# A decoder block's gate and up products: one pair of k-tiles by seven block products instead of eight

## The chip, the core and the metric

The kernel runs on one core of a Trainium2 chip. The metric is the device time of one execution in microseconds (us); less is better. The engines are PE (TensorE: matmuls, and PEld for its weight loads), DVE (VectorE), ACT (ScalarE), POOL (GpSimd) and SP (SyncE, which here issues the loads of weights).

## What is computed

A decoder block on 256 tokens of width 2048 in float32: attention and an mLSTM side by side, a SwiGLU feed-forward stage, and a gated per-layer embedding. What the change touches is the first half of the feed-forward stage, with weights of 2048 x 5632:

```python
h2 = rms_norm(x, w_norm_ffn[i])
x = x + (jax.nn.silu(h2 @ w_ffn_gate[i]) * (h2 @ w_ffn_up[i])) @ w_ffn_down[i]
gate = jax.nn.sigmoid(rms_norm(x, w_norm_ple[i]) @ w_ple_gate[i])
```

## The kernel before

**Split operands.** The matmuls take operands of type fp32r. Each operand is a sum of two parts: a cast by ACT (wh, act_h) and the rest by a DVE subtraction (wl, act_l). A product takes three matmuls, high x high, high x low and low x high (lines 255 to 257), each with a 128x128 block of activations as weights of PE and 512 columns of the weight matrix streaming through it. The activations lie transposed, contraction on the partitions: a "k-tile" is 128 of the 2048 contraction rows, a "block" b is 128 of the 256 tokens.

**One linear (lines 210 to 258).** It walks over pieces of two k-tiles. SP loads a piece of 128x1024 floats (wr), ACT casts it (L230), DVE subtracts (L231), and PE multiplies each of its k-tiles with both blocks into two PSUM banks (acc0, acc1): 12 matmuls for each piece. wr, wh and wl have four buffers each. PSUM has four names (acc0, acc1, tr, sc) with two banks each, eight in all.

**Feed-forward (lines 644 to 659).** The 5632 columns are 11 chunks of 512. A chunk is a linear for gate, per block a sigmoid by ACT (L650) and a DVE product (L651), a linear for up, and per block one more DVE product (L654): 2 x 16 x 2 x 3 = 192 matmuls. Then a task turns the chunk's result into activations for the down product: DVE transposes of 32x32 into "tq" (L187), four POOL DMAs to DRAM ("swap", L191), one back into "quad" (L196), then cast and subtraction (L129, L130). "tq" and "quad" have one buffer each, and a list `held` lets one task at a time use them. The activations of the chunk before the first (acts_h, four quarters of four k-tiles) are made in the same way after each quarter of the attention output product; PE needs the last quarter for k-tiles 12 to 15.

**What sets the order.** Python writes the instructions in order; the background tasks write a step whenever `advance` is called, once for each piece here. A planner then puts each engine's instructions in an order of its own: on each engine it takes the earliest written one that is ready by its estimate of the times. On the chip that order is fixed: a DVE or ACT instruction that waits holds everything queued behind it.

**Before down.** Lines 660 to 664 load p, transpose it on PE and split it, between the last chunk and the first down piece. `e_norm` loads w_ple_post into one buffer (wpost, L679).

Of the kernel before, what the change touches and what calls it, by code (L numbers as in the profile page):

```python
# [19 lines left out]
def block_kernel(ctx, tc, x, p, w_norm_mix, w_in, fox_f_bias, q_norm_w, k_norm_w, conv_w, conv_b,  # L20
# [180 lines left out]
    def split_by_blocks(dst, srcs, scales=None, gap=2):  # L201
# [5 lines left out]
                yield  # L207
        held.pop()

    def linear(w, acts, c0, n, pieces=None, before=None, load=None, width=2):  # L210

        po = [ps.tile([P, 512], F32, name=f"acc{b}") for b in range(2)]
        total = w.shape[0] // P
        if pieces is None:
            step = 1024 // n if n < 512 else 2
            pieces = [(k, min(step, total - k)) for k in range(0, total, step)]
        count = 0
        ready = []

        def fetch(i):  # L220
            kt, nk = pieces[i]
            if load is not None:
                load(kt)

            def piece(name, dt):
                return wpool.tile([P, 1024], dt, name=name)[:, 0:nk * n].rearrange("p (k n) -> p k n", k=nk)

            wr, wh, wl = piece("wr", F32), piece("wh", F32R), piece("wl", F32R)
            nc.sync.dma_start(out=wr, in_=w[kt * P:(kt + nk) * P, c0:c0 + n].rearrange("(k p) n -> p k n", p=P))
            nc.scalar.copy(wh, wr)  # L230
            nc.vector.tensor_tensor(wl, wr, wh.bitcast(F32), op=ALU.subtract)  # L231
            ready.append((wh, wl))

        for i, (kt, nk) in enumerate(pieces):
            if before is None:
                advance(width)
                fetch(i)
            else:
                if i == 0:
                    fetch(0)  # L240
                    before(kt)
                if i + 1 < len(pieces):
                    fetch(i + 1)
                if i:
                    before(kt)
            wh, wl = ready[i]
            for j in range(nk):
                ah, al = acts[(kt + j) // 4]
                while id(ah) in made_by and not made_by[id(ah)].done:
                    advance(2)  # L250
                kk = (kt + j) % 4
                count += 1
                for b in range(2):
                    s = slice(b * P, (b + 1) * P)
                    nc.tensor.matmul(po[b][:, 0:n], ah[:, kk, s], wh[:, j, :], start=count == 1, stop=False)  # L255
                    nc.tensor.matmul(po[b][:, 0:n], ah[:, kk, s], wl[:, j, :], start=False, stop=False)  # L256
                    nc.tensor.matmul(po[b][:, 0:n], al[:, kk, s], wh[:, j, :], start=False, stop=count == total)  # L257
        return [t[:, 0:n] for t in po]


    with tc.tile_pool(name="mixp", bufs=1) as mp:
# [52 lines left out]
        def qk_norm(s, dT, vec):  # L314
            ss = small.tile([P, 2, 4], F32, name="ss_qk")
            rr = small.tile([P, 2, 4], F32, name="r_qk")
            for b in range(2):
                sq = small.tile([P, 512], F32, name="sqf", bufs=1)
# [319 lines left out]
    with tc.tile_pool(name="ffnp", bufs=1) as fp:  # L638
        acts_g = []

        def after_up(dst, gg):
            yield from split_by_blocks(dst, lambda b: gg[b])

        for c in range(NG):
            pg = linear(w_gate, acts_h, c * 512, 512, width=1)
            gg = [None, None]
            for b in range(2):
                gg[b] = fp.tile([P, 512], F32, name=f"gg{b}", bufs=2)
                r = rstd2[:, b:b + 1]
                nc.scalar.activation(gg[b], pg[b], AF.Sigmoid, scale=r)  # L650
                nc.vector.scalar_tensor_tensor(gg[b], pg[b], r, gg[b], op0=ALU.mult, op1=ALU.mult)  # L651
            pu = linear(w_up, acts_h, c * 512, 512, width=1)
            for b in range(2):
                nc.vector.scalar_tensor_tensor(gg[b], pu[b], rstd2[:, b:b + 1], gg[b], op0=ALU.mult, op1=ALU.mult)  # L654
# [5 lines left out]
        p_sb = fp.tile([P, 512], F32, name="gg0", bufs=2).rearrange("p (b k) -> p b k", b=2)  # L660
        nc.sync.dma_start(out=p_sb, in_=p.rearrange("(b p) k -> p b k", p=P))
        acts_p = (fp.tile([P, 2, 256], F32R, name="ph"), fp.tile([P, 2, 256], F32R, name="pl"))
        for _ in transpose_in(acts_p, lambda b, j: p_sb[:, b, j * P:(j + 1) * P], 0, 2):
            pass
        e = []

        def e_norm():
            ss_e = const.tile([P, 2, 4], F32, name="ss_e")
            rstd_e = const.tile([P, 2], F32, name="rstd_e")
            for c in range(4):  # L670
                for b in range(2):
                    sumsq(ss_e[:, b, c:c + 1], e[c][:, b, :])
                yield
            ssr = small.tile([P, 2], F32, name="ssr")
            nc.vector.tensor_reduce(ssr, ss_e, axis=AX.X, op=ALU.add)
            rsqrt(rstd_e, ssr, 1.0 / D, [P, 2])
            for c in range(4):
                cs = slice(c * 512, (c + 1) * 512)
                wpost = fp.tile([P, 512], F32, name="wpost")  # L679
                nc.sync.dma_start(out=wpost, in_=w_ple_post[0, cs].partition_broadcast(P))  # L680
                for b in range(2):
                    yield
                    nc.vector.scalar_tensor_tensor(e[c][:, b, :], e[c][:, b, :], rstd_e[:, b:b + 1], wpost,
                                                   op0=ALU.mult, op1=ALU.mult)

        def e_chunks():
            for c in range(4):
                po = linear(w_ple_proj, [acts_p], c * 512, 512)
                e.append(act.tile([P, 2, 512], F32, name="act_h"))
                for b in range(2):  # L690
                    nc.scalar.copy(e[c][:, b, :], po[b])
            Task(e_norm())

        order = [(k, 2) for k in list(range(16, 4 * NG, 2)) + list(range(0, 16, 2))]
        acts_h3, rstd3 = residual(w_down, acts_g, v_ple, "ple", pieces=order)


        e_chunks()
        out_v = out.rearrange("(b p) n -> p b n", p=P)
        for c0, n in ((0, 512), (512, 512), (1024, 512), (1536, 256), (1792, 256)):  # L700
            cs = slice(c0, c0 + n)
            po = linear(w_ple_gate, acts_h3, c0, n)
            for b in range(2):
                g = fp.tile([P, 512], F32, name=f"gg{b}", bufs=2)[:, 0:n]
# [32 lines left out]
```

## Time and profile before

| | us |
|---|---|
| median of 3 runs (1227.53 to 1228.53) | 1228.31 |
| the profiled execution | 1228.32 |
| its span, first to last instruction | 1226.6 |
| PE / DVE / ACT busy | 1215.5 / 713.4 / 585.9 |

Times are counted from the start of the span. PE's busy time counts pipelined matmuls that overlap, so it says when PE has something to do, not that it is at its peak; the distance between the starts of neighbouring matmuls says that. In the waits, "A <- B" is an engine's line that stood still until B's was done, and the idle time of an engine that is not the bottleneck costs nothing. In a timeline, a bracket tells how long the engine stood before the instruction, and what released it; "x2" is two of them merged. Gate and up run from 400 to 880 us.

### The profile page before, as it was taken

To read this page: it belongs to the slowest core of one execution; us is meant where nothing else is said; L and a number is where in the kernel's file an instruction comes from. 1 tells how busy PE (TensorE), PEld (TensorE's weight loads), DVE (VectorE), ACT (ScalarE), POOL (GpSimd) and SP (SyncE) were. 2 spreads that over 40 slices of the span, in tenths; PEclk is the share of its full clock that TensorE was granted. 3 is DMA by queue.
4 is the path that set the end of the run, shared out by engine and by line. 5 is a ranking of instruction groups with operands and counts; after the bars stand their busy time and mean duration, and the time that the engine had idled before them with its cause. 6 is when DMAs were issued, how large, how long until landed. Compare 5 with 4: busy or idle time off the path is not lost.

```text
span 1226.6 us, 15283 instructions
## 1 busy us (share of the span) xinstructions
PE 1215.5 (99%) x5675; PEld 1018.3 (83%) x5675; DVE 713.4 (58%) x956; ACT 585.9 (48%) x766; POOL 79.5 (6%) x149
## 2 busy tenths in 40 slices
PE   8999999999999999999999999999999999999998
PEld 6899978878888788888888888888888888888888
DVE  5766755665656655555565565555545554545754
ACT  6655556545545444444444444444444444446542
POOL 1111000000010000000000000000000000000000
PEclk9999999999999999999999999999999999999999
DMA  7677744675677776776776677677666666665672
GB/s 260 205 237 230 231 139 130 177 236 170 207 247 243 222 223 197 233 223 195 230 228 209 209 231 226 191 230 229 210 212 208 213 208 212 205 212 168 220 248 90
DMA packets 136383, 257.32 MB, mean 210 GB/s; under 512 B 10002, under 2 KB 29300, under 8 KB 136308
## 3 DMA queue, kind: packets, MB, share of 16 engines
q1 hardware_dynamic: 127156, 229.06, 59.6%
q0 software_dynamic: 8400, 26.22, 6.8%
q8 instruction: 44, 0.72, 0.2%
q10 hardware_dynamic: 752, 1.06, 0.2%
q14 instruction: 31, 0.25, 0.1%
HBM read 241.10 MB, written 15.20 MB: 209 GB/s over the span
## 4 chain that ended last, share of the span: by engine, by line
PE 91%; DMA 4%; DVE 2%; ACT 1%; issue 1%; POOL 0%; SPq 0%; DVEq 0%; ACTq 0%; POOLq 0%
PE acc L256 30%; PE acc L255 30%; PE acc L257 30%; DMA quad<-swap 2%; DMA wr<-in_w_in_dram 1%; DVE wl L231 1%; DMA swap<-tq 1%; ACT wh L230 0%; PE tr L165 0%; POOL swap L191 0%; PE sc L552 0%; PE tr L569 0%; DVE tq L187 0%; PE sc L505 0%; PE tr L489 0%
## 5 line engine op out<-in xcount | busy, mean ns | idle before, releaser
L231 DVE TENSOR_TENSOR wl<-wr,wh 128x1024 fp32r<-128x1024 f32 (+2 forms) x445 | 525.0, 1182 | 435.9 <-ACT wh L230 434.8
L230 ACT CAST wh<-wr 128x1024 fp32r<-128x1024 f32 (+2 forms) x445 | 452.2, 1019 | 558.1 <-PE acc L257 522.8
L255 PE MATMUL acc<-wh,act_h 128*128 128x512 f32 (+2 forms) x1568 | 594.0, 379 | 2.3 <-ACT act_h L133 2.3
L256 PE MATMUL acc<-wl,act_h 128*128 128x512 f32 (+2 forms) x1568 | 591.1, 377 | 1.2 <-DVE wl L231 1.2
L257 PE MATMUL acc<-wh,act_l 128*128 128x512 f32 (+2 forms) x1568 | 591.3, 377 | 0.0
L255 PEld LDWEIGHTS acc<-wh,act_h 128*128 128x128 f32 x1568 | 294.8, 188 | 54.5 <-ACT act_h L133 3.5
L256 PEld LDWEIGHTS acc<-wl,act_h 128*128 128x128 f32 x1568 | 294.8, 188 | 52.1 <-DVE wl L231 1.9
L257 PEld LDWEIGHTS acc<-wh,act_l 128*128 128x128 f32 x1568 | 294.7, 188 | 52.0 <-DVE act_l L135 0.8
L191 POOL DMA_DIRECT2D swap<-tq x100 | 61.0, 616 | 877.0 <-DVE tq L187 877.0
L255 PE MATMUL acc<-wh,gh 128*128 128x512 f32 x224 | 88.0, 393 | 0.0
L256 PE MATMUL acc<-wl,gh 128*128 128x512 f32 x224 | 87.9, 393 | 0.0
L257 PE MATMUL acc<-wh,gl 128*128 128x512 f32 x224 | 87.1, 389 | 0.0
L257 PEld LDWEIGHTS acc<-wh,gl 128*128 128x128 f32 x224 | 42.0, 188 | 9.5
L255 PEld LDWEIGHTS acc<-wh,gh 128*128 128x128 f32 x224 | 42.1, 188 | 9.4
L256 PEld LDWEIGHTS acc<-wl,gh 128*128 128x128 f32 x224 | 42.1, 188 | 8.6
L196 POOL DMA_DIRECT2D quad<-swap x25 | 14.0, 559 | 114.0 <-DMA swap<-tq 69.1
L650 ACT ACTIVATE gg<-acc,rstd_ffn 128x512 f32<-128x512 f32 x22 | 15.1, 689 | 10.8 <-PE acc L257 10.8
L651 DVE SCALAR_TENSOR_TENSOR gg<-acc,rstd_ffn,gg 128x512 f32<-128x512 f32 x22 | 15.8, 751 | 5.0 <-ACT gg L650 5.0
L133 ACT ACTIVATE act_h<-quad,vec_b 128x256 fp32r<-128x256 f32 x32 | 13.7, 498 | 4.5 <-DMA quad<-swap 4.3
L654 DVE SCALAR_TENSOR_TENSOR gg<-acc,rstd_ffn,gg 128x512 f32<-128x512 f32 x22 | 15.4, 744 | 0.0
L135 DVE SCALAR_TENSOR_TENSOR act_l<-quad,vec_b,act_h 128x256 fp32r<-128x256 f32 x32 | 13.4, 480 | 2.9 <-ACT act_h L133 2.9
L116 ACT ACTIVATE sq<-xres 128x512 bf16<-128x512 f32 x24 | 14.9, 623 | 0.0
(194 smaller groups left out, 405.1 us busy)
## 6 DMA issues: line engine op xcount, KB each, us to landing
wr<-in_w_ffn_gate_dram SPq DMA_DIRECT2D x88, 512.0 KB, 3.8
wr<-in_w_ffn_up_dram SPq DMA_DIRECT2D x88, 512.0 KB, 4.5
wr<-in_w_ffn_down_dram SPq DMA_DIRECT2D x88, 512.0 KB, 4.0
wr<-in_w_in_dram SPq DMA_DIRECT2D x63, 512.0 KB, 4.7
wr<-in_w_in_dram SPq DMA_DIRECT2D x48, 344.0 KB, 3.7
wr<-in_w_out_dram SPq DMA_DIRECT2D x32, 512.0 KB, 4.5
wr<-in_w_ple_gate_dram SPq DMA_DIRECT2D x32, 512.0 KB, 4.7
swap<-tq POOLq DMA_DIRECT2D x100, 128.0 KB, 4.4
```

The lines of the kernel that those rows point to most:

```text
L116: nc.scalar.activation(sq[:, 0:n], src, AF.Square, accum_out=dst)
L133: nc.scalar.activation(part(dst[0], k + j, 1), src[:, j:j + 1], AF.Copy, scale=scales[j])
L191: nc.gpsimd.dma_start(out=d[:, :, :, i, :].rearrange("j c b e -> c b j e"), in_=t[32 * i:32 * i + 32].rearrange("c b j k r -> c b j (k r)"))
L196: nc.gpsimd.dma_start(out=q.rearrange("p t k r -> p (t k r)"), in_=d.rearrange("j c b i e -> (j c) (b i e)"))
L230: nc.scalar.copy(wh, wr)
L231: nc.vector.tensor_tensor(wl, wr, wh.bitcast(F32), op=ALU.subtract)
L255: nc.tensor.matmul(po[b][:, 0:n], ah[:, kk, s], wh[:, j, :], start=count == 1, stop=False)
L256: nc.tensor.matmul(po[b][:, 0:n], ah[:, kk, s], wl[:, j, :], start=False, stop=False)
L257: nc.tensor.matmul(po[b][:, 0:n], al[:, kk, s], wh[:, j, :], start=False, stop=count == total)
L650: nc.scalar.activation(gg[b], pg[b], AF.Sigmoid, scale=r)
L651: nc.vector.scalar_tensor_tensor(gg[b], pg[b], r, gg[b], op0=ALU.mult, op1=ALU.mult)
L654: nc.vector.scalar_tensor_tensor(gg[b], pu[b], rstd2[:, b:b + 1], gg[b], op0=ALU.mult, op1=ALU.mult)
```

## The change

Gate and up of a chunk are now done together (`gate_up`). A pair of k-tiles is a unit: its gate and up pieces side by side are a 2x2 block matrix (rows: the two k-tiles, columns: gate and up), and the activations of the pair another (rows: the two token blocks, columns: the k-tiles). Seven of the eight pairs are multiplied plainly, in eight block products. One pair, k-tiles 2 and 3 (`seven = (1,)`), which comes fifth in the first chunk and fourth in the others, is multiplied by Strassen's scheme (in Winograd's form): seven products P1 to P7 of sums of blocks. The sums of the activations are made once by a task (`make_forms`, into fh and fl), those of the weights in every chunk by DVE (`seven_unit`: t12, t34, in a two-buffer tile "wt"), and each is cast and split like a piece (`halves`), in 3.5 pieces instead of 2. The plain products go straight into the banks of P2, P3, P4 and P8; P1, P5, P6 and P7 have four banks of their own, are read in mid chunk (`t1`, `qr`, `su`) and added to the others at the chunk's end. The four shared banks and the four own ones change names from chunk to chunk. `qr` lies in "quad" and `su` in "tq". gg0 and gg1 have one buffer instead of two, p is loaded and transposed by a task during the down product, sqf moves to another pool, and wpost gets two buffers.

```diff
+    def halves(wr):
+        k, n = wr.shape[1:]
+        wh, wl = (wpool.tile([P, 1024], F32R, name=name)[:, 0:k * n].rearrange("p (k n) -> p k n", k=k)
+                  for name in ("wh", "wl"))
+        nc.scalar.copy(wh, wr)
+        nc.vector.tensor_tensor(wl, wr, wh.bitcast(F32), op=ALU.subtract)
+        return wh, wl
...
-            wr, wh, wl = piece("wr", F32), piece("wh", F32R), piece("wl", F32R)
-            nc.sync.dma_start(out=wr, in_=w[kt * P:(kt + nk) * P, c0:c0 + n].rearrange("(k p) n -> p k n", p=P))
-            nc.scalar.copy(wh, wr)
-            nc.vector.tensor_tensor(wl, wr, wh.bitcast(F32), op=ALU.subtract)
-            ready.append((wh, wl))
+            ready.append(halves(load_piece(w, kt, nk, c0, n)))
...
+        seven = (1,)
+        first_order, later_order = (0, 2, 3, 4, 1, 5, 6, 7), (0, 2, 3, 1, 4, 5, 6, 7)
+        def make_forms(p):
+            while held:
+                yield held
+            held.append(p)
...
+            fa = quads.tile([P, 2, 2, P], F32, name="tq")
...
+            nc.vector.tensor_tensor(fa.rearrange("p k b t -> p k (b t)"), h[:, k:k + 2, :].bitcast(F32),
+                                    l[:, k:k + 2, :].bitcast(F32), op=ALU.add)
+            yield
+            f = quads.tile([P, 4, P], F32, name="quad")
...
+            nc.vector.scalar_tensor_tensor(f[:, 0], a21, -1.0, a22, op0=ALU.mult, op1=ALU.subtract)
+            nc.vector.scalar_tensor_tensor(f[:, 1], f[:, 0], -1.0, a11, op0=ALU.mult, op1=ALU.subtract)
+            nc.vector.tensor_tensor(f[:, 2], a11, a21, op=ALU.subtract)
+            nc.vector.tensor_tensor(f[:, 3], a12, f[:, 1], op=ALU.subtract)
+            yield
+            nc.scalar.copy(fh, f)
+            nc.vector.tensor_tensor(fl, f, fh.bitcast(F32), op=ALU.subtract)
...
+        def plain_unit(c, p, acts):
+            w2 = [halves(load_piece(w, 2 * p, 2, c * 512, 512)) for w in (w_gate, w_up)]
...
+        def seven_unit(c, p):
+            ra, rb = (load_piece(w, 2 * p, 2, c * 512, 512) for w in (w_gate, w_up))
+            t12 = fp.tile([P, 2, 512], F32, name="wt", bufs=2)
+            nc.vector.tensor_tensor(t12[:, 0], ra[:, 0], rb[:, 0], op=ALU.subtract)
+            nc.vector.tensor_tensor(t12[:, 1], t12[:, 0], rb[:, 1], op=ALU.add)
+            t34 = fp.tile([P, 2, 512], F32, name="wt", bufs=2)
+            nc.vector.tensor_tensor(t34[:, 0], t12[:, 1], ra[:, 0], op=ALU.subtract)
+            nc.vector.tensor_tensor(t34[:, 1], ra[:, 1], t12[:, 1], op=ALU.subtract)
+            ah, al = halves(ra)
+            h12, l12 = halves(t12)
+            bh, bl = halves(rb[:, 1:2])
+            h34, l34 = halves(t34)
+            right = {"P1": (ah[:, 0], al[:, 0]), "P6": (h12[:, 1], l12[:, 1]), "P5": (h12[:, 0], l12[:, 0]),
+                     "P2": (ah[:, 1], al[:, 1]), "P7": (h34[:, 0], l34[:, 0]), "P4": (h34[:, 1], l34[:, 1]),
+                     "P3": (bh[:, 0], bl[:, 0])}
...
+        def gate_up(c):
+            own, shared = (("acc0", "acc1"), ("tr", "sc"))[::1 - 2 * (c % 2)]
+            tags = {"P1": own[0], "P6": own[0], "P7": own[1], "P5": own[1],
+                    "P2": shared[0], "P3": shared[1], "P4": shared[0], "P8": shared[1]}
...
+                for n, (lh, ll), (rh, rl) in unit:
...
+                    nc.tensor.matmul(bank[n], lh, rh, start=first, stop=False)
+                    nc.tensor.matmul(bank[n], lh, rl, start=False, stop=False)
+                    nc.tensor.matmul(bank[n], ll, rh, start=False, stop=left[n] == 0)
+                if su is None and left["P1"] == 0:
+                    while held:
+                        advance(1)
+                    t1 = fp.tile([P, 512], F32, name="sg", bufs=2)
+                    nc.scalar.copy(t1, bank["P1"])
+                    qr = quads.tile([P, 2, 512], F32, name="quad")
+                    nc.vector.tensor_tensor(qr[:, 0], bank["P6"], t1, op=ALU.add)
+                    nc.vector.tensor_tensor(qr[:, 1], bank["P7"], qr[:, 0], op=ALU.add)
+                    su = quads.tile([P, 2, 512], F32, name="tq")
+                    for i in range(2):
+                        nc.vector.tensor_tensor(su[:, i], bank["P5"], qr[:, i], op=ALU.add)
+            gg = [fp.tile([P, 512], F32, name=f"gg{b}") for b in range(2)]
+            nc.vector.tensor_tensor(gg[0], bank["P2"], t1, op=ALU.add)
+            nc.vector.tensor_tensor(gg[1], bank["P4"], qr[:, 1], op=ALU.add)
+            nc.vector.tensor_tensor(su[:, 0], bank["P3"], su[:, 0], op=ALU.add)
+            nc.vector.tensor_tensor(su[:, 1], bank["P8"], su[:, 1], op=ALU.add)
+            for b in range(2):
+                r = rstd2[:, b:b + 1]
+                sg = fp.tile([P, 512], F32, name="sg", bufs=2)
+                nc.scalar.activation(sg, gg[b], AF.Sigmoid, scale=r)
+                nc.vector.scalar_tensor_tensor(gg[b], gg[b], r, sg, op0=ALU.mult, op1=ALU.mult)
+                nc.vector.scalar_tensor_tensor(gg[b], su[:, b], r, gg[b], op0=ALU.mult, op1=ALU.mult)
...
+        def load_p():
+            yield
+            yield
+            p_sb = fp.tile([P, 512], F32, name="gg0").rearrange("p (b k) -> p b k", b=2)
+            nc.sync.dma_start(out=p_sb, in_=p.rearrange("(b p) k -> p b k", p=P))
+            for _ in range(6):
+                yield
+            yield from transpose_in(acts_p, lambda b, j: p_sb[:, b, j * P:(j + 1) * P], 0, 2)
```

## Rows read from the trace of the kernel before

**Rows 1.** The page: busy us (share of span) xinstructions; chain that ended last.

```profile
PE 1215.5 (99%) x5675; PEld 1018.3 (83%) x5675; DVE 713.4 (58%) x956; ACT 585.9 (48%) x766; POOL 79.5 (6%) x149
...
PE 91%; DMA 4%; DVE 2%; ACT 1%; issue 1%; POOL 0%; SPq 0%; DVEq 0%; ACTq 0%; POOLq 0%
```

**Rows 2.** The waits, whole span: who for whom; us in total, times, longest.

```profile
ACT wh L230 <- PE acc L257: 522.8, 336, 4.0
DVE wl L231 <- ACT wh L230: 434.8, 343, 5.6
...
ACT gh L129 <- DMA quad<-swap: 4.5, 3, 2.0
```

**Rows 3.** Timeline of ACT, sigmoids of two chunks: start, us, engine, line, operation.

```profile
509.87 1.37 ACT L650 ACTIVATE gg<-acc,rstd_ffn 128x512 f32<-128x512 f32 x2 [0.99 <-PE acc L257]
...
858.02 1.37 ACT L650 ACTIVATE gg<-acc,rstd_ffn 128x512 f32<-128x512 f32 x2 [0.98 <-PE acc L257]
```

**Rows 4.** Timeline of PE at one of them.

```profile
857.60 0.39 PE L257 MATMUL acc<-wh,act_l 128*128 128x512 f32 x1
857.83 0.39 PE L255 MATMUL acc<-wh,act_h 128*128 128x512 f32 x1
858.05 0.39 PE L256 MATMUL acc<-wl,act_h 128*128 128x512 f32 x1
```

**Rows 5.** Timeline of PE in the first chunk.

```profile
416.44 0.39 PE L257 MATMUL acc<-wh,act_l 128*128 128x512 f32 x1
417.65 0.50 PE L255 MATMUL acc<-wh,act_h 128*128 128x512 f32 x1 [0.82 <-ACT act_h L133]
```

**Rows 6.** The chain of waits by time, 398 to 418 us: start, us, what.

```profile
404.78 5.03 DMA swap<-tq
...
410.40 6.67 DMA quad<-swap
```

**Rows 7.** Groups by line, 400 to 880 us: line engine op out<-in, count | busy us, mean ns.

```profile
L231 DVE TENSOR_TENSOR wl<-wr,wh 128x1024 fp32r<-128x1024 f32 x177 | 216.4, 1223 | 200.0 <-ACT wh L230 200.0
L230 ACT CAST wh<-wr 128x1024 fp32r<-128x1024 f32 x176 | 185.5, 1054 | 252.1 <-PE acc L257 251.6 <-ACT sq L116 0.5
L257 PEld LDWEIGHTS acc<-wh,act_l 128*128 128x128 f32 x705 | 132.3, 188 | 27.7 <-DVE act_l L135 0.2
...
L654 DVE SCALAR_TENSOR_TENSOR gg<-acc,rstd_ffn,gg 128x512 f32<-128x512 f32 x21 | 14.8, 744 | 0.0
...
L130 DVE TENSOR_TENSOR gl<-quad,gh 128x512 fp32r<-128x512 f32 x12 | 7.7, 686 | 1.3 <-ACT gh L129 1.3
L129 ACT CAST gh<-quad 128x512 fp32r<-128x512 f32 x12 | 6.8, 618 | 2.5 <-DMA quad<-swap 2.5
...
L629 DVE TENSOR_TENSOR xres<-acc,xres 128x512 f32<-128x512 f32 x2 | 1.3, 682 | 0.0
```

**Rows 8.** Busy time by stretch: stretch us, PE, PEld, DVE, ACT, POOL, PEclk, DMA share, GB/s.

```profile
120.00:140.00 20.00, 19.18 (x122) 18.89 (x121) 17.03 (x30) 12.03 (x17) 0.00 (x0) 1.00 0.66 181
240.00:260.00 20.00, 20.00 (x90) 16.56 (x89) 14.96 (x26) 11.57 (x15) 2.99 (x5) 1.00 0.63 201
509.87:553.39 43.52, 43.52 (x193) 36.04 (x192) 24.65 (x25) 19.17 (x21) 3.00 (x5) 1.00 0.71 219
```

**Rows 9.** Timeline of DVE at a chunk's end.

```profile
531.82 1.40 DVE L654 SCALAR_TENSOR_TENSOR gg<-acc,rstd_ffn,gg 128x512 f32<-128x512 f32 x2
533.13 1.30 DVE L187 STREAM_TRANSPOSE tq<-gg 128x512 f32<-128x512 f32 x2
534.35 1.19 DVE L231 TENSOR_TENSOR wl<-wr,wh 128x1024 fp32r<-128x1024 f32 x1
536.11 1.23 DVE L231 TENSOR_TENSOR wl<-wr,wh 128x1024 fp32r<-128x1024 f32 x1 [0.58 <-ACT wh L230]
```

**Rows 10.** Timeline of PE at 123 us, in the first stretch of these.

```profile
123.47 0.42 PE L256 MATMUL acc<-wl,act_h 128*128 128x344 f32 x1 [0.81 <-DVE wl L231]
```

**Rows 11.** DMA issues: out<-in, queue, count, KB each, median us to landing.

```profile
wr<-in_w_ffn_gate_dram SPq DMA_DIRECT2D x88, 512.0 KB, 3.8
```

More of the change, by code (lines that the diff above doesn't have):

```diff
@@ L208, in split_by_blocks, with load_piece @@
         held.pop()
+    def load_piece(w, kt, nk, c0, n):
+        wr = wpool.tile([P, 1024], F32, name="wr")[:, 0:nk * n].rearrange("p (k n) -> p k n", k=nk)
+        nc.sync.dma_start(out=wr, in_=w[kt * P:(kt + nk) * P, c0:c0 + n].rearrange("(k p) n -> p k n", p=P))
+        return wr
+    def halves(wr):
[5 more added lines that the diff above has]
+        return wh, wl
     def linear(w, acts, c0, n, pieces=None, before=None, load=None, width=2):
@@ L317, in qk_norm @@
             for b in range(2):
-                sq = small.tile([P, 512], F32, name="sqf", bufs=1)
+                sq = mp.tile([P, 512], F32, name="sqf")
                 nc.scalar.activation(sq, s[:, b, :], AF.Square)
@@ L642, in after_up @@
             yield from split_by_blocks(dst, lambda b: gg[b])
-        for c in range(NG):
[L645 to L654, printed above, removed]
+        seven = (1,)
@@ new lines, in block_kernel @@
+        first_order, later_order = (0, 2, 3, 4, 1, 5, 6, 7), (0, 2, 3, 1, 4, 5, 6, 7)
+        forms = {}
+        def make_forms(p):
+            while held:
+                yield held
+            held.append(p)
+            h, l = acts_h[p // 2]
+            k = 2 * (p % 2)
+            fa = quads.tile([P, 2, 2, P], F32, name="tq")
+            fh = fp.tile([P, 4, P], F32R, name=f"fh{p}")
+            fl = fp.tile([P, 4, P], F32R, name=f"fl{p}")
+            nc.vector.tensor_tensor(fa.rearrange("p k b t -> p k (b t)"), h[:, k:k + 2, :].bitcast(F32),
+                                    l[:, k:k + 2, :].bitcast(F32), op=ALU.add)
+            yield
+            f = quads.tile([P, 4, P], F32, name="quad")
+            a11, a12, a21, a22 = fa[:, 0, 0], fa[:, 1, 0], fa[:, 0, 1], fa[:, 1, 1]
+            nc.vector.scalar_tensor_tensor(f[:, 0], a21, -1.0, a22, op0=ALU.mult, op1=ALU.subtract)
[5 more added lines that the diff above has]
+            nc.vector.tensor_tensor(fl, f, fh.bitcast(F32), op=ALU.subtract)
+            forms[p] = {"P1": (h[:, k, 0:P], l[:, k, 0:P]), "P2": (h[:, k + 1, 0:P], l[:, k + 1, 0:P]),
+                        "P4": (h[:, k + 1, P:2 * P], l[:, k + 1, P:2 * P]),
+                        **{n: (fh[:, i], fl[:, i]) for i, n in enumerate(("P5", "P6", "P7", "P3"))}}
+            held.pop()
+            yield
@@ new lines, in plain_unit @@
+        def plain_unit(c, p, acts):
+            w2 = [halves(load_piece(w, 2 * p, 2, c * 512, 512)) for w in (w_gate, w_up)]
+            out = []
+            for j in range(2):
+                h, l = acts
+                k = 2 * (p % 2) + j
+                for b in range(2):
+                    t = slice(b * P, (b + 1) * P)
+                    for i in range(2):
+                        out.append((("P2", "P3", "P4", "P8")[2 * b + i], (h[:, k, t], l[:, k, t]),
+                                    (w2[i][0][:, j, :], w2[i][1][:, j, :])))
+            return out
@@ new lines, in seven_unit @@
+        def seven_unit(c, p):
[13 more added lines that the diff above has]
+                     "P3": (bh[:, 0], bl[:, 0])}
+            return [(n, forms[p][n], v) for n, v in right.items()]
@@ new lines, in gate_up @@
+        def gate_up(c):
+            own, shared = (("acc0", "acc1"), ("tr", "sc"))[::1 - 2 * (c % 2)]
+            tags = {"P1": own[0], "P6": own[0], "P7": own[1], "P5": own[1],
+                    "P2": shared[0], "P3": shared[1], "P4": shared[0], "P8": shared[1]}
+            order = first_order if c == 0 else later_order
+            left = {"P1": len(seven), "P6": len(seven), "P7": len(seven), "P5": len(seven), "P8": 16 - 2 * len(seven),
+                    **{n: 16 - len(seven) for n in ("P2", "P3", "P4")}}
+            bank, t1, qr, su = {}, None, None, None
+            for p in order:
+                advance(1)
+                if p in seven:
+                    while p not in forms:
+                        advance(1)
+                    unit = seven_unit(c, p)
+                else:
+                    h = acts_h[p // 2]
+                    unit = plain_unit(c, p, h)
+                    while id(h[0]) in made_by and not made_by[id(h[0])].done:
+                        advance(2)
+                advance(1)
+                for n, (lh, ll), (rh, rl) in unit:
+                    first = n not in bank
+                    if first:
+                        bank[n] = ps.tile([P, 512], F32, name=tags[n])
+                    left[n] -= 1
+                    nc.tensor.matmul(bank[n], lh, rh, start=first, stop=False)
[3 more added lines that the diff above has]
+                    while held:
+                        advance(1)
+                    t1 = fp.tile([P, 512], F32, name="sg", bufs=2)
[4 more added lines that the diff above has]
+                    su = quads.tile([P, 2, 512], F32, name="tq")
+                    for i in range(2):
+                        nc.vector.tensor_tensor(su[:, i], bank["P5"], qr[:, i], op=ALU.add)
[4 more added lines that the diff above has]
+            nc.vector.tensor_tensor(su[:, 1], bank["P8"], su[:, 1], op=ALU.add)
+            for b in range(2):
+                r = rstd2[:, b:b + 1]
[3 more added lines that the diff above has]
+                nc.vector.scalar_tensor_tensor(gg[b], su[:, b], r, gg[b], op0=ALU.mult, op1=ALU.mult)
+            return gg
@@ L655, in block_kernel @@
+        for c in range(NG):
+            if c == 0:
+                for kp in seven:
+                    Task(make_forms(kp), [made_by[id(acts_h[kp // 2][0])]])
+            gg = gate_up(c)
             if c < 4:
@@ L659, in block_kernel @@
             made_by[id(acts_g[c][0])] = Task(after_up(acts_g[c], gg))
[L660 to L664, printed above, removed]
+        acts_p = [fp.tile([P, 2, 256], F32R, name="wt", bufs=2) for _ in range(2)]
+        def load_p():
[4 more added lines that the diff above has]
+            for _ in range(6):
+                yield
+            yield from transpose_in(acts_p, lambda b, j: p_sb[:, b, j * P:(j + 1) * P], 0, 2)
+        made_by[id(acts_p[0])] = Task(load_p())
         e = []
@@ L678, in e_norm @@
                 cs = slice(c * 512, (c + 1) * 512)
-                wpost = fp.tile([P, 512], F32, name="wpost")
+                wpost = fp.tile([P, 512], F32, name="sg", bufs=2)
                 nc.sync.dma_start(out=wpost, in_=w_ple_post[0, cs].partition_broadcast(P))
@@ L703, in block_kernel @@
             for b in range(2):
-                g = fp.tile([P, 512], F32, name=f"gg{b}", bufs=2)[:, 0:n]
+                g = fp.tile([P, 512], F32, name=f"gg{b}")[:, 0:n]
                 nc.scalar.activation(g, po[b], AF.Sigmoid, scale=rstd3[:, b:b + 1])
```

2 lines of the change are left out of this document (removed).

## The prediction

> **What bounds the kernel now.** I read the page's shares of engines first: PE is busy for 1215.5 of 1226.6 us, DVE for 58% and ACT for 48%, and the chain that ended last is 91% PE [rows 1]. A busy PE need not be a full one, so the waits came next: ACT's casts of weights waited 522.8 us in 336 places for PE, that is, for PE to give a buffer back, and DVE's subtractions waited for those casts [rows 2]. Both helpers are ahead of PE and held by its buffers. Then the beat: the first sigmoids of two chunks, eight chunks apart, start at 509.87 and 858.02 us [rows 3], so a chunk lasts 348.15 / 8 = 43.519 us; it has 192 matmuls of 512 columns, 0.2267 us each. Neighbouring matmuls in the trace start 0.22 to 0.23 us apart [rows 4]. So gate and up are nothing but matmuls in a row, at granted clock 1.00 (2.4 GHz, the upper of its two levels) [rows 8], and a matmul that is left out gives back 0.2267 us if what feeds PE keeps up. PE's starts show one hole in this stage: the matmul after 416.44 us came at 417.65 [rows 5], 1.21 - 0.23 = 0.98 us late. The chain names its cause: the last quarter of acts_h comes by two DMA trips of 5.03 and 6.67 us and landed at 417.07 [rows 6].
>
> **The change, part by part.** *Matmuls.* A plain unit (one pair of k-tiles, gate and up) has 2 k-tiles x 2 blocks x 2 matrices x 3 = 24 matmuls, the seven products 7 x 3 = 21. One pair of eight per chunk: 3 fewer, 11 chunks, 33 x 0.2267 = **-7.48 us**. *The hole of chunk 0.* Before, the pieces that need the last quarter come after 72 matmuls. In the new order (0, 2, 3, 4, 1, 5, 6, 7) they come after 96 + 21 + 24 = 141, 32 us after the start: **-0.98 us**. What is late next is make_forms, which needs the same "quad" buffer once that quarter is split: landing at 417.07, four casts and subtractions, then three short steps, about 5 us by pieces like those of [rows 7], so near 422; chunk 0 starts at 417.65 - 0.98 - 16.32 = 400.35, its second product P6 at 400.35 + 99 x 0.2267 = 422.8. One loss of 0 to 1 us; I take 0, since P1 and P2 need no form.
>
> A rule of the Trainium skill prices the first term otherwise. In the rows, one weight load takes 188 ns of the 226.7 ns beat [rows 4, 7], 83%. Perfetto Trace Analysis, section Identifying the Most-Contended Engine, says that for TensorE the share of weight loads tells the distance to the limit and matmul occupancy doesn't; by that, 33 loads of 0.188 would be worth 6.2 us, 1.3 less. The beat of rows 3 decides here, and the trace sides with it: nothing waits between those matmuls.
>
> *DVE.* Per chunk it gains: one subtraction of 1024 columns (1.22 us) and one of 512 (0.69); four sums of weights from SBUF (0.69 each, by the two-input form of 512 columns); four sums from PSUM in mid chunk and four at the end (0.68 each, by xres <- acc) [rows 7]. The four scalar_tensor_tensor stay. 1.91 + 2.74 + 2.73 + 2.73 = 10.1 us on 24.65 of 43.52 [rows 8]: 34.8 of 42.84, 81% instead of 57%. *ACT*: casts of 1.05 and 0.62 and a copy of 0.62, 19.17 + 2.3 = 21.5, 50%. Neither becomes the bound on average. The cost is a matter of places, and there are two.
>
> *Place 1, after the seven products.* That unit takes all four wh and wl buffers, so the next unit's pieces wait for its products. A reader of PE's result starts about 0.42 us after the last matmul's start (857.60 to 858.02) [rows 3, 4]. Count from its first matmul: P5 ends its use of a buffer with the matmul at 1.81, P2 with that at 2.49. Gate: cast 2.23 to 3.28, subtraction to 4.5, wanted at 4.99 (22 matmuls). Up: cast 3.28 to 4.33, subtraction to 5.7, wanted at 5.67. Just in time; if ACT's copy of P1 or one or two of the mid-chunk sums come first, 0.6 to 0.8 us late.
>
> *Place 2, the chunk's end.* Before, two DVE operations and two transposes stood there (531.82 to 534.35 us) [rows 9], and the next piece's buffer had come free three pieces, 8.2 us, ahead of its use. Now a unit uses both its pieces to the end, so the second unit's pieces get their buffers just as the chunk begins (0) and are wanted at 5.67 and 6.35. P4's sum can start at -0.49; from there DVE has two sums (0.68), four scalar_tensor_tensor (0.66 apart) and two transposes (0.61 apart), to 4.7, and only then, if it goes in written order, the subtractions: 5.9 and 7.2. Late by 0.3 and 0.5, 0.8 together. If the planner lets the subtractions pass the transposes (which have to wait for "tq", now held by su), nothing is late.
>
> So the bounds of this unknown are 0 and 0.8 + 0.8 = 1.6 us per chunk; a gain I exclude, as PE has no other wait to lose here. No row shows this crowd; the nearest are stretches where DVE is as busy: at 75% (240 to 260 us) PE lost nothing, at 85% (120 to 140) it lost 0.82 of 20 us [rows 8], at one late subtraction [rows 10]. 81% lies between, and only about a third of a chunk is crowded: I take 0.2 us per chunk, 11 x 0.2 = **+2.2 us**.
>
> *Nothing for the rest.* PSUM: the banks that chunk c+1 sums into from its start were the own banks of chunk c, read in mid chunk, some 10 us or more before; without that cover PE would wait 2 to 3 us per chunk for the end sums. DMA: the same bytes in 1.6% less time, DMA share 0.71 [rows 8]; a piece lands 3.8 us after its issue [rows 11] and is asked for about two units of 5.4 us ahead. p is loaded by a task into gg0, which now has one buffer: on SP's queue weights of the down stage may stand behind it until the last transposes have read gg0, some 5 us, with four loaded pieces (10.9 us) in hand: 0; if it issued later than planned, 1 to 2 us once. Its transposes on PE only move. The new helpers, sqf's pool and two buffers for wpost change no matmul's inputs in time.
>
> **Sum** against the profiled execution's own time, 1228.32 us (span 1226.6 and 1.7 around it; the median of the runs is 1228.31, the same): 1228.32 - 7.48 - 0.98 + 2.2 = 1222.06, **1222.0 us**.
>
> **Rivals.** *A, the crowd eats the gain.* If the two places cost 8.46 / 11 = 0.77 us per chunk, half of their bound, the time is 1228.3: no change. For it: the hand count has no margin in either place. Against: planned stretches at 75% without loss. A sentence of the skill fits its picture: Perfetto Trace Analysis, same section, reads the same gap repeating as too few buffers for the next tile; no such gap is in the trace of before. *B, slower: the round trip.* The mid-chunk sums write qr into "quad", which the previous chunk's activations hold until their trip through DRAM has landed and been split. That trip starts after the transposes, now about 5 us into the chunk instead of 2, and took 11.7 us and more by DMA alone [rows 6]: the buffer comes free about 20 us into the chunk, where the seven products end (21). DVE takes its instructions in order; if qr's sums, or the split behind the landing, are queued ahead of subtractions and the landing is later than planned, weights wait behind a DMA. In the kernel before, ACT stood 4.5 us in three places for this landing [rows 2], without harm since PE had three pieces in hand. It decides from about 1 us of lateness; at 1.5 us per chunk the sum is 1219.9 + 16.5 = 1236. Against: three times of eleven, and at most 2.0 us, is what the trace shows. *C, no loss at all*: 1219.9. That fewer products run is no doubt; that the forms of chunk 0 come late costs at most 1 us and lies in the range.
>
> **Chances.** Forecast, 0 to 0.5 us lost per chunk (1219.9 to 1225.4, C at its lower edge): 0.62; a little faster still by something I don't see, below 1219: 0.03; between forecast and no change: 0.02. A (1225.9 to 1230.8): 0.16. B (above 1230.8): 0.17. Two in ten may be left out: 1219.0 to 1231.5 leaves some 0.03 below and 0.15 above. Over 0.2% (2.5 us), about what a measurement of this kernel can tell from no change: faster 0.67, within 0.16, slower 0.17.
>
> **What would show it.** Right: chunks 42.84 us apart plus at most a few tenths, 189 matmuls in each, no hole near 417 us, DVE near 81%. PE's holes tell which place costs: about 22 us into a chunk on a wl of the unit behind the seven (place 1), 5 to 7 us into it (place 2), or with ACT or DVE standing for quad<-swap (B). Wrong: matmuls of the seven products further apart than 0.2267 us, or holes of over 0.8 us in every chunk.

## The result and the profile after

The changed kernel takes 1242.07 us, the median of 4 executions (1239.55 to 1245.13), against 1227.92 us for the kernel before (4 executions, 1227.1 to 1228.53): a ratio of 1.0118, 95% interval 1.0101 to 1.0135. It is slower, outside the predicted range of 1219.0 to 1231.5. The profiled execution takes 1245.13 us, its span is 1243.4.

The page of the kernel after, its shares of engines and the chain that ended last:

```profile
PE 1217.0 (98%) x5642; PEld 1015.1 (82%) x5642; DVE 810.4 (65%) x1116; ACT 602.3 (48%) x800; POOL 79.5 (6%) x149
...
PE 72%; DMA 12%; DVE 7%; issue 4%; ACT 3%; POOL 2%; SPq 0%; POOLq 0%; DVEq 0%; ACTq 0%
```

PE has fewer matmuls than in [rows 1] and yet 1.5 us more busy time, and the chain is 72% PE where it was 91%: DMA rose from 4% to 12%. The waits of the whole span say where (who for whom; us in total, times, longest):

```profile
POOL quad L196 <- DMA swap<-tq: 106.5, 19, 6.6
...
ACT gh L129 <- DMA quad<-swap: 11.4, 7, 3.1
PEld acc L742 <- ACT wh L220: 10.3, 5, 4.4
...
ACT act_h L129 <- DMA quad<-swap: 9.6, 4, 4.2
...
PE acc L742 <- ACT wh L220: 8.2, 5, 3.9
PE sc L742 <- ACT wh L220: 7.8, 5, 3.1
```

ACT's split of a chunk's activations waits for the trip through DRAM in all 11 chunks, 21.0 us together, instead of 4.5 us in three [rows 2]. And PE, which never did, waits for a cast of weights (L220): ten times, one hole in each chunk but the first. The longest hole is in the second chunk; here it is on PE first, then on ACT (start, us, engine, line, operation; the bracket is the idle time before and its releaser):

```profile
464.70 0.40 PE L744 MATMUL acc<-wh,act_l 128*128 128x512 f32 x1
469.03 1.22 PE L742 MATMUL acc<-wh,act_h 128*128 128x512 f32 x2 [3.94 <-ACT wh L220]
```

```profile
461.65 1.05 ACT L220 CAST wh<-wr 128x1024 fp32r<-128x1024 f32 x1 [0.20 <-PE sc L744]
466.90 1.14 ACT L129 CAST act_h<-quad 128x512 fp32r<-128x512 f32 x2 [4.19 <-DMA quad<-swap]
467.94 2.94 ACT L220 CAST wh<-wr 128x1024 fp32r<-128x1024 f32 x3
```

464.70 is the third matmul of the plain unit behind the seven products. These three use its gate piece, cast at 461.65; the next needs its up piece, and that cast, with two more, is queued behind the split, which stands 4.19 us for "quad". PE's next matmul comes 4.33 us after the last, 4.10 more than the beat of 0.23. Without the wait the split (1.04 us to the next start) and the up cast (1.05) would have been done at 464.8, just when PE wanted it: nothing was in hand, so the holes follow the waits:

| chunk | 1 | 2 | 3 | 4 | 5 | 6 | 7 | 8 | 9 | 10 |
|---|---|---|---|---|---|---|---|---|---|---|
| ACT's split waits for the landing, us | 4.19 | 3.24 | 1.22 | 0.91 | 0.32 | 0.92 | 1.82 | 2.51 | 1.61 | 1.13 |
| PE's hole in the unit behind the seven products, us | 4.10 | 3.21 | 1.19 | 0.89 | 0.31 | 0.89 | 1.80 | 2.49 | 1.59 | 1.11 |

They agree to 0.1 us, and the holes add up to 17.6 us. (ACT's eleventh wait, 3.1 us, lies behind the stage, in the down product, and PE has no hole there.) The chain of waits gives the trip of the second chunk (start, us, what):

```profile
449.35 0.68 DVE tq L187
...
450.44 1.83 POOL swap L191 x3
452.26 6.43 DMA swap<-tq
...
459.43 7.45 DMA quad<-swap
...
466.90 0.03 ACT act_h L129
```

The chunk began near 442.8 (399.41 for the stage, 189 matmuls of 0.2267, 0.57 lost in the first chunk). The transposes end 7.2 us into it, the trip's two DMAs take 13.9 us together, and the landing is 24 us into the chunk; the seven products end at 21.4 (464.24).

Behind the longest hole the clock fell too. Busy time by stretch (stretch, its length, PE, PEld, DVE, ACT, POOL, granted clock, DMA share, GB/s):

```profile
463.00:466.00 3.00, 2.10 (x10) 1.36 (x8) 0.97 (x1) 0.00 (x0) 0.00 (x0) 1.00 0.59 178
466.00:469.00 3.00, 0.00 (x0) 0.00 (x0) 1.29 (x2) 2.10 (x4) 0.00 (x0) 0.87 0.34 130
469.00:472.00 3.00, 2.97 (x7) 2.39 (x8) 2.99 (x4) 1.88 (x2) 0.00 (x0) 0.50 0.22 33
472.00:475.00 3.00, 3.00 (x8) 2.32 (x8) 2.90 (x4) 0.00 (x0) 0.00 (x0) 0.50 0.86 281
475.00:478.00 3.00, 3.00 (x14) 2.45 (x14) 0.65 (x1) 1.74 (x2) 0.00 (x0) 0.99 0.66 216
```

From 469 to 475 us the granted clock is 0.50, that is 1.2 GHz, and matmuls start 0.43 us apart. The 15 from 469.03 on took 6.34 us instead of 3.40: 2.9 us more. The holes of 3.21 and 2.49 us are followed by the same, 1.8 and 1.7 us more.

The stage is the clean measure, since where it begins differs by some us between executions: from the first matmul of gate and up to the first of down it lasts 497.64 us (399.41 to 897.05), against 480.28 before (400.35 to 880.63). 2079 matmuls of 0.22667 are 471.25. Of the 26.4 us above that, the ten holes are 17.6, the slow clock 6.4, a late matmul of the first chunk 0.6; 1.8 us are spread thin.

### The profile page after: what moved, and what is told of

It is laid out like the page before. It is cut to its first block, busy times and chain, and to the rows that moved or that the text cites. A ratio compares the mean times of both kernels' runs of the same rounds, so it can differ in the third digit from the quotient of the medians.

```text
span 1243.4 us, 15436 instructions
## 1 busy us (share of the span) xinstructions
PE 1217.0 (98%) x5642; PEld 1015.1 (82%) x5642; DVE 810.4 (65%) x1116; ACT 602.3 (48%) x800; POOL 79.5 (6%) x149
## 4 chain that ended last, share of the span: by engine, by line
PE 72%; DMA 12%; DVE 7%; issue 4%; ACT 3%; POOL 2%; SPq 0%; POOLq 0%; DVEq 0%; ACTq 0%
PE acc L263 16%; PE acc L262 16%; PE acc L264 16%; DMA quad<-swap 6%; DMA swap<-tq 5%; PE acc L742 3%; PE acc L743 3%; PE acc L744 3%; PE sc L742 2%; PE tr L742 2%; PE tr L744 2%; PE tr L743 2%; PE sc L743 2%; PE sc L744 2%; ACT wh L220 2%
## 5 line engine op out<-in xcount | busy, mean ns | idle before, releaser
L221 DVE TENSOR_TENSOR wl<-wr,wh 128x1024 fp32r<-128x1024 f32 (+2 forms) x445 | 513.7, 1166 | 318.5 <-ACT wh L220 317.7
L220 ACT CAST wh<-wr 128x1024 fp32r<-128x1024 f32 (+2 forms) x445 | 440.4, 1007 | 502.8 <-PE acc L264 260.4
L262 PE MATMUL acc<-wh,act_h 128*128 128x512 f32 (+2 forms) x864 | 320.1, 371 | 1.4 <-ACT act_h L133 1.4
L263 PE MATMUL acc<-wl,act_h 128*128 128x512 f32 (+2 forms) x864 | 317.2, 367 | 0.9 <-DVE wl L221 0.8
L264 PE MATMUL acc<-wh,act_l 128*128 128x512 f32 (+2 forms) x864 | 317.4, 367 | 0.0
L262 PEld LDWEIGHTS acc<-wh,act_h 128*128 128x128 f32 x864 | 162.7, 188 | 25.8 <-ACT act_h L133 1.9
L263 PEld LDWEIGHTS acc<-wl,act_h 128*128 128x128 f32 x864 | 162.7, 188 | 24.3 <-DVE wl L221 1.6
L264 PEld LDWEIGHTS acc<-wh,act_l 128*128 128x128 f32 x864 | 162.5, 188 | 24.3 <-DVE act_l L135 0.6
L742 PE MATMUL acc<-wh,act_h 128*128 128x512 f32 x296 | 114.5, 395 | 8.2 <-ACT wh L220 8.2
L743 PE MATMUL acc<-wl,act_h 128*128 128x512 f32 x296 | 116.3, 393 | 0.0
L744 PE MATMUL acc<-wh,act_l 128*128 128x512 f32 x296 | 116.2, 392 | 0.0
L742 PEld LDWEIGHTS acc<-wh,act_h 128*128 128x128 f32 x296 | 55.8, 190 | 21.8 <-ACT wh L220 10.3
L742 PE MATMUL tr<-wh,act_h 128*128 128x512 f32 x185 | 72.7, 393 | 0.0
```

The lines of the kernel that those rows point to most:

```text
L742: nc.tensor.matmul(bank[n], lh, rh, start=first, stop=False)
L743: nc.tensor.matmul(bank[n], lh, rl, start=False, stop=False)
L744: nc.tensor.matmul(bank[n], ll, rh, start=False, stop=left[n] == 0)
```

## The experiments

All edits are to the changed kernel, and a line of it can have a number a few higher in an edited one (L753 and L223 of a_split_tq are its L751 and L221). The theory: the split, queued on ACT ahead of weights and waiting for the trip, makes the holes (rival B of the prediction). Against it stood that the crowd of DVE sums makes them, that units of two pieces with swapped banks cost by themselves, and that taking one waiter away might only bring out the next. "Lost" is the time of the stage above its matmuls; the ratios of the edited kernels are to 19 executions of the kernel before, taken beside them (median 1227.46 or 1227.80).

| kernel | gate and up to down, us | its matmuls x 0.22667 | lost, us | ratio to before, 95% |
|---|---|---|---|---|
| before | 480.28 | 478.7 | 1.6 | |
| changed | 497.64 | 471.3 | 26.4 | 1.0118 (1.0101 to 1.0135) |
| d_plain | 478.76 | 478.7 | 0.0 | 0.9994 (0.9980 to 1.0008) |
| a_split_tq | 512.06 | 471.3 | 40.8 | 1.0229 (1.0173 to 1.0285) |
| e_no_wait | 473.64 | 471.3 | 2.4 | 0.9962 (0.9948 to 0.9976) |
| b_order | 473.78 | 471.3 | 2.5 | 0.9960 (0.9945 to 0.9976) |
| c_behind5 | 478.85 | 471.3 | 7.6 | 0.9993 (0.9983 to 1.0002) |
| g_fifth | 478.36 | 471.3 | 7.1 | 0.9996 (0.9983 to 1.0010) |
| g_seventh | 480.72 | 471.3 | 9.5 | 1.0044 (1.0029 to 1.0059) |
| f_two | 496.59 | 463.8 | 32.8 | 1.0148 (1.0123 to 1.0172) |

**Without the seven products (d_plain).** All eight pairs are plain; units of two pieces and the swap of banks stay.

```diff
-        seven = (1,)
+        seven = ()
...
-            nc.vector.tensor_tensor(gg[0], bank["P2"], t1, op=ALU.add)
...
+            for b, (pg, pu) in enumerate((("P2", "P3"), ("P4", "P8"))):
```

> The changed kernel with no pair by seven products: eight plain units per chunk, gate and up side by side, banks swapping as in the change, 192 matmuls, no sums. Theory 1 (trip): the trip starts about 3 us earlier in the chunk and the weights behind its landing are a plain unit's, so no holes: 1227 to 1229 us (1228.3 less the hole of the first chunk). Theory 2 (crowd, by units of two pieces): the plain units alone lose some of it, 1231 us or more.

1227.56 us (10 executions). Busy time of one stretch of this stage, columns as above:

```profile
440.00:483.00 43.00, 43.00 (x191) 35.63 (x190) 24.18 (x24) 18.51 (x20) 3.00 (x5) 1.00 0.69 219
```

PE is full at a granted clock of 1.00 and the stage is its matmuls to 0.1 us, though ACT waited for the landing of five chunks in this stage, 2.3 us at most (and 5.1 us for the last one, behind it). So the new order of pieces and banks is free, and a wait of ACT alone doesn't make a hole.

**ACT's wait taken away (a_split_tq).** The split reads "tq" itself, so it waits for no trip; the trip is still made. The planner then puts the split earlier in the queues too, at 452.55 us for the second chunk, ahead of the seven products. (The activations of the down product get their elements from the wrong places.)

```diff
+        if direct:
+            return t.rearrange("p b j k c -> p k (b j) c")
         return q.rearrange("p t k r -> p k t r")
...
-            yield from split_by_blocks(dst, lambda b: gg[b])
+            yield from split_by_blocks(dst, lambda b: gg[b], direct=True)
```

> The changed kernel, but the cast and subtraction that make the down product's activations read the tile tq (the transposes' own output) instead of quad, where the trip through DRAM lands; the trip is still made. So these activations hold the wrong elements, and only the wait for the landing is gone. Theory 1 (trip): in the changed kernel ACT's queue holds the weights of the unit behind the seven products back behind a cast that waits for quad<-swap, once per chunk; PE's hole there (0.3 to 4.1 us, 17.6 us in ten chunks) and the halved clock after the long ones go with it: 1220 to 1224 us, no hole over 0.5 us. Theory 2 (crowd): the holes come from buffers and DVE's load around the seven products: 1238 to 1245 us as before.

1260.24 us (4 executions, 1248.08 to 1262.08), slower still and outside what either theory gave: a miss. The waits, then DVE and PE in one of the late chunks:

```profile
DVE quad L753 <- DMA quad<-swap: 19.8, 8, 3.8
```

```profile
837.61 0.69 DVE L753 TENSOR_TENSOR quad<-tr,sg 128x512 f32<-128x512 f32 x1 [3.77 <-DMA quad<-swap]
838.39 0.69 DVE L757 TENSOR_TENSOR tq<-sc,quad 128x512 f32<-128x512 f32 x1
838.99 0.68 DVE L754 TENSOR_TENSOR quad<-sc,quad 128x512 f32<-128x512 f32 x1
839.59 1.22 DVE L223 TENSOR_TENSOR wl<-wr,wh 128x1024 fp32r<-128x1024 f32 x1
```

```profile
836.07 1.07 PE L744 MATMUL acc<-wh,act_h 128*128 128x512 f32 x4
840.86 0.79 PE L745 MATMUL acc<-wl,act_h 128*128 128x512 f32 x1 [3.73 <-DVE wl L223]
```

ACT's wait is gone and DVE has it: the first sum of qr, which writes "quad", waits for the same landing, with sums and the subtraction (L223) that PE needs behind it. It stands 1.2 to 3.8 us in each of the ten chunks behind the first (in two of them the view names another releaser than the landing), and PE's hole behind it is 0.1 us longer each time. These ten holes add up to 26.4 us, and behind six of them the clock fell. The change had put two instructions that need the landing ahead of weights, one on each engine; in the changed kernel ACT's was merely the first.

**Both waiters taken away (e_no_wait).** As in a_split_tq, and qr in a buffer of its own.

```diff
-                    qr = quads.tile([P, 2, 512], F32, name="quad")
+                    qr = fp.tile([P, 2, 512], F32, name="qr")
```

> The changed kernel in its own order (seven products fourth), with both waiters of the trip's landing gone: the activations of the down product are split from tq (they hold the wrong elements; the trip is still made), and qr lies in a tile of its own instead of quad. Theory 1 (an instruction that waits for quad<-swap stands ahead of weights in ACT's or DVE's queue): nothing stands there any more; gate and up take 471.3 to 475 us (before 480.3, changed 497.6), 1220 to 1224 us in all, no fall of the clock. Theory 2 (crowd around the seven products): holes of over 1 us per chunk stay, 1235 us or more.

1223.78 us (10 executions), faster than before. Busy time in the stage:

```profile
449.00:492.00 43.00, 43.00 (x190) 35.36 (x189) 33.14 (x39) 20.83 (x24) 2.99 (x5) 1.00 0.69 220
```

PE is full. Every sum, cast and subtraction of the change is still there, though the split stands earlier in the queues, as in a_split_tq; 2.4 us are lost in the stage instead of 26.4. With the table of waits and holes above and b_order below, which keeps the split as it is, that settles the cause: the waits for the trip, on both queues, and not the work of DVE.

**One constant (b_order).** The seven products come sixth instead of fourth in all chunks but the first. Nothing else.

```diff
-        first_order, later_order = (0, 2, 3, 4, 1, 5, 6, 7), (0, 2, 3, 1, 4, 5, 6, 7)
+        first_order, later_order = (0, 2, 3, 4, 1, 5, 6, 7), (0, 2, 3, 4, 5, 1, 6, 7)
```

> One constant: in the chunks after the first the seven products come sixth instead of fourth, (0, 2, 3, 4, 5, 1, 6, 7). By the queue that results, the waiting cast now stands ahead of the seven's own weights and behind the plain units' ones. Theory 1 (trip): the landing, 24.5 us into the chunk, is wanted a unit later than before; holes of 0 to 1 us per chunk, 1220 to 1230 us, ACT's wait for quad<-swap well under the 21.0 us of the changed kernel. Theory 2 (crowd): the hole moves with the seven products to the place behind them and stays as large: 1238 to 1245 us.

1223.55 us (4 executions, 1222.27 to 1225.03): faster than both kernels. The waits, ACT in the second chunk, and the busy time around that wait:

```profile
ACT gh L129 <- DMA quad<-swap: 23.5, 7, 3.6
...
ACT act_h L129 <- DMA quad<-swap: 13.0, 4, 3.5
```

```profile
462.07 2.01 ACT L220 CAST wh<-wr 128x1024 fp32r<-128x1024 f32 x2 [3.39 <-PE acc L744]
467.33 1.15 ACT L129 CAST act_h<-quad 128x512 fp32r<-128x512 f32 x2 [3.25 <-DMA quad<-swap]
468.38 1.05 ACT L220 CAST wh<-wr 128x1024 fp32r<-128x1024 f32 x1
469.99 1.05 ACT L220 CAST wh<-wt 128x1024 fp32r<-128x1024 f32 x1 [0.56 <-DVE wt L703]
```

```profile
466.00:472.00 6.00, 6.00 (x28) 4.99 (x27) 4.11 (x7) 3.15 (x4) 0.00 (x0) 1.00 0.56 186
```

ACT waits longer than in the changed kernel, 36.5 us instead of 21.0, in every chunk (well under 21.0 was expected, a miss), and PE doesn't notice. When ACT stops at 464.1, two pieces of the fifth unit are cast (462.07), and the sixth starts near 473; its first cast is done at 469.4. The wait stands where a plain unit of 5.4 us covers it. The place of the wait in the queue decides whether its length costs PE anything: behind the seven products each microsecond did, here none does.

**The split queued further back (c_behind5).** b_order, with more steps between the parts of the trip and the split tied behind the last cast written ahead of it.

```diff
-            yield from split_by_blocks(dst, lambda b: gg[b])
+            yield from split_by_blocks(dst, lambda b: gg[b], gap=5, behind=True)
```

> As the one with the seven products sixth, and the cast that waits for quad<-swap is written later (gap 5) and tied behind the last cast of the seven's weights in ACT's queue, some 28 us into the chunk, when the trip has landed. Theory 1 (trip): ACT's wait for quad<-swap is about 0, no hole over 0.5 us per chunk, no fall of the clock: 1219.9 to 1223 us, faster than the kernel before. Theory 2 (crowd): holes behind the seven products stay, over 1235 us.

1226.99 us (10 executions): no chunk's split waits for its landing any more but the last one's, 0.7 us, and yet it is slower than b_order and than the 1219.9 to 1223 expected, a miss. Its waits:

```profile
ACT wh L229 <- DMA wr<-in_w_ffn_gate_dram: 26.1, 9, 3.0
ACT wh L229 <- DMA wr<-in_w_ffn_up_dram: 24.9, 18, 3.4
```

ACT now waits for weights, 51.0 us, of which the changed kernel showed 2.2 us in this stage and b_order 10.2, and PE loses about 0.1 us many times in the unit behind the seven products, and 0.75 and 0.60 us once each at a late wl. Whether these waits of ACT cause PE's losses, and what makes the weights later, was not found out.

**Fifth and seventh place (g_fifth, g_seventh).** Again the one constant: (0, 2, 3, 4, 1, 5, 6, 7) and (0, 2, 3, 4, 5, 6, 1, 7).

> The changed kernel with the seven products fifth in all chunks. By the queue that results, the cast that waits for the landing (some 21.1 us into the chunk) stands ahead of the last two casts of the seven's own weights, which PE wants 24.7 us into the chunk. Theory 1: two casts and a subtraction after 22.2 us end near 25.1: holes of about 0.4 us at P7, at most 1: 1222 to 1229 us. Theory 2: the same as in the changed kernel, 1238 to 1245 us.

> The changed kernel with the seven products seventh in the chunks after the first. The cast that waits for the landing stands among casts of plain units, a unit of 5.4 us ahead of their use. Theory 1: as with the seven products sixth, 1222 to 1226 us. Theory 2: 1238 to 1245 us; and the mid-chunk sums, now some 38 us into the chunk, may hold up the next chunk's banks: above the sixth place by 1 us per chunk.

g_fifth takes 1226.14 us (10 executions), inside the 1222 to 1229 that was expected: losses of 0.3 to 0.6 us at P7's wl in five chunks, and of 0.1 to 0.2 us behind the seven products in most. g_seventh takes 1233.07 (4 executions), above the 1222 to 1226 that was expected, by about the microsecond per chunk that the expectation allowed for late banks; but no bank is late. There the mid-chunk sums fall onto the sums of the chunk's end, and DVE is late with wl for the second unit of the next chunk (place 2 of the prediction): PE stands for it 0.2 to 1.2 us in nearly every chunk, and the last time, already in the down product, 1.5 us:

```profile
888.13 0.63 PE L262 MATMUL acc<-wh,gh 128*128 128x512 f32 x2
890.30 0.51 PE L263 MATMUL acc<-wl,gh 128*128 128x512 f32 x1 [1.54 <-DVE wl L221]
```

So of the four places tried, the sixth is the only one that is clear of the trip ahead and the chunk's end behind.

**Two pairs by seven products (f_two).** `seven = (1, 3)`, both late in the chunk.

> Two pairs by seven products (k-tiles 2, 3 and 6, 7), sixth and seventh in the chunks after the first, fifth and sixth in the first: 186 matmuls per chunk, another 33 x 0.2267 = 7.5 us less, and about 7 us more of DVE's time per chunk (some 98% of a chunk). Theory 1 with my crowd term: without a waiter in a tight place the crowd costs what DVE can't do in time; at 98% I expect it to eat the gain and more: 1224 to 1245 us. If DVE's load costs as little as with one pair: 1216 to 1219 us.

1246.62 us (4 executions), 1.6 us above the 1224 to 1245 that was expected. 33 more matmuls are gone, but 32.8 us are lost, 3 us per chunk, most of it where PE stands for wl. PE, and a stretch of one chunk:

```profile
853.66 0.61 PE L742 MATMUL tr<-wh,act_h 128*128 128x512 f32 x2
855.28 0.50 PE L743 MATMUL sc<-wl,act_h 128*128 128x512 f32 x1 [1.01 <-DVE wl L221]
```

```profile
807.00:853.00 46.00, 44.55 (x193) 35.43 (x192) 38.66 (x47) 23.09 (x26) 2.99 (x5) 1.00 0.68 213
```

DVE is 84% busy, not the 98% expected, and 76% with one pair (32.83 of 43 us in b_order, 446 to 489 us). Ahead of the hole shown it has worked without a gap since 829 us, so here the crowd of rival A is real. It need not be all: ACT also waits 107.8 us for weights of gate and up, in b_order 10.2, and 27.5 us for landings, and no run separates the three.

## Why the prediction was wrong

*Matmuls, -7.48 us.* Right. Where nothing waits the beat is unchanged (d_plain: 478.76 us for 2112), and e_no_wait's 473.64 is 5.1 less, 7.5 less 2.4.

*The hole of chunk 0, -0.98, and the forms, 0 to 1.* Right: no matmul is late near 417 us, and 0.57 us are lost at the second product, the place foreseen. But the form (fh) was in time; late was the subtraction of that product's weights (wl), which DVE made behind the forms' sums. (b_order has the same first chunk and no such loss.) PE in the changed kernel:

```profile
421.85 0.40 PE L742 MATMUL acc<-wh,fh 128*128 128x512 f32 x1
422.65 0.50 PE L743 MATMUL acc<-wl,fh 128*128 128x512 f32 x1 [0.41 <-DVE wl L221]
```

*DVE and the crowd, +2.2.* Right in size, as e_no_wait and b_order show: 2.4 and 2.5 us of the stage, 0.2 per chunk. In part that is luck, since DVE comes to 76% rather than the 81% from which it was read off. The two places cost next to nothing where the kernel has its seventh and its second unit in good time: in b_order a loss of 0.11 us right behind the seven products stands in ten chunks, and nothing larger. With that rival A falls, and rival C, which had no loss at all.

*The round trip, rival B.* This is the failed step: the sum put the wait for the trip at nothing, and the stage lost 17.6 us by it in holes and 6.4 us by the clock behind them. The mechanism was named, and its condition: the split or qr's sums queued ahead of weights, and a late landing. It was given 0.17 because the trace of before showed three waits of eleven, 2.0 us at most [rows 2], and that row was the wrong evidence. It was taken with the trip starting 3 us into a chunk and with three pieces in hand behind it. POOL in the second chunk of the kernel before, which began near 444.85 us:

```profile
447.80 2.44 POOL L191 DMA_DIRECT2D swap<-tq  x4 [36.85 <-DVE tq L187]
454.41 0.56 POOL L196 DMA_DIRECT2D quad<-swap  x1 [4.17 <-DMA swap<-tq]
```

Both were about to change, and the prediction's own text said so. Two terms of its count were off in the same direction, and a third followed from them:

- The trip's start was set at 5 us into the chunk. It was 7.6 (450.44 less 442.8): two subtractions (at 445.79 and 447.59) passed the transposes on DVE, which the prediction had named as what would save place 2. What saved the weights there made the trip later. DVE after the end sums of the first chunk, with the second of them:

```profile
446.93 0.74 DVE L766 SCALAR_TENSOR_TENSOR gg<-tq,rstd_ffn,gg 128x512 f32<-128x512 f32 x1
447.59 1.22 DVE L221 TENSOR_TENSOR wl<-wr,wh 128x1024 fp32r<-128x1024 f32 x1
448.73 1.30 DVE L187 STREAM_TRANSPOSE tq<-gg 128x512 f32<-128x512 f32 x2
```

- The trip was priced by the two DMAs of [rows 6], 5.03 and 6.67. They took 6.43 and 7.45 in the second chunk, and from the first issue of a chunk's trip to that of its last DMA it was 8.4 to 9.2 us, before 6.5 to 7.1. Part comes with paired units, as d_plain shows (7.3 to 8.8); the rest is open.
- So the buffer was free 24 us into the second chunk, not 20, and the margin of 1 us before the seven products' end, which the text itself worked out, was a deficit of 2.6. With nothing in hand behind it, each us that the split waited was a us of PE.

B's price, 1.5 us per chunk, was close for the holes (17.6 / 11 = 1.6). It left out what PE's clock adds, 6.4 us. 1219.9 + 17.6 + 6.4 + 0.6 = 1244.5, and with the thin losses of 1.8 it would be 1246.3 against 1245.13 measured; most of the difference is in where the stage begins, 0.9 us earlier here.

*The sentence of the Trainium skill.* The prediction set beside rival A that the same gap repeating can mean too few buffers for the next tile (the Trainium skill, Perfetto Trace Analysis; it stands in section Optimization Strategy, the one behind the section that the prediction names). The gap did repeat, once per chunk. One more buffer (e_no_wait, for qr, beside a split that reads "tq") goes with its end, but b_order ends it with the same buffers by moving work: the traces bear the sentence out only as far as its "can".

Not tried: qr in its own buffer with the split as it is, and a shorter trip.

## What to carry to other kernels

Before moving work behind a round trip, list on each in-order queue every instruction that waits for the landing, and ask of each what is queued behind it and how many microseconds of the bottleneck's work are in hand there; an old trace's short waits say nothing once the trip starts later or the hand is smaller. Take away one waiter and the next one takes its place (a_split_tq), so look for a place in the order where all of them are covered: here one constant turned a ratio of 1.012 into 0.996. DVE's average share (76% in b_order) doesn't tell which of the two a kernel will get.

## What the hardware showed that was not expected

A long hole of PE cost more than its length. In the changed kernel, after holes of 4.10, 3.21 and 2.49 us the granted clock went to 0.50 (1.2 GHz), matmuls of 512 columns started 0.43 instead of 0.227 us apart for some 4 to 6 us, and 2.9, 1.8 and 1.7 us were added. After the holes of 1.80 us and less it stayed at 1.00; these two stretches, columns as above, hold those of 1.19 and 1.59 us:

```profile
560.00:566.00 6.00, 4.96 (x22) 3.79 (x21) 4.61 (x6) 4.55 (x6) 0.00 (x0) 1.00 0.56 180
828.00:834.00 6.00, 4.57 (x20) 3.45 (x19) 4.82 (x6) 3.99 (x5) 0.00 (x0) 1.00 0.49 165
```

But the length of the hole alone doesn't decide it. In a_split_tq the clock stayed at 1.00 behind a hole of 2.40 us and fell behind one of 2.31 us, eight matmuls starting 0.43 us apart; each stretch begins where the hole ends:

```profile
650.90:656.90 6.00, 5.92 (x26) 4.89 (x27) 4.64 (x6) 1.05 (x1) 0.00 (x0) 1.00 0.74 215
743.90:749.90 6.00, 5.95 (x19) 4.73 (x20) 4.00 (x4) 0.15 (x1) 0.00 (x0) 0.72 0.71 212
```
